# RMSNorm with SiLU on one core: three slots of eight rows instead of six of four, with loads on SyncE and stores on ScalarE

## The chip, the cores and the metric

The kernel runs on one core of a Trainium2 chip. The metric is the device time of one execution, in microseconds (us). Before the change three executions took 316.73, 316.79 and 317.04 us; the median, 316.79 us, is the time before.

The engines that matter here are VectorE (DVE in the profile), ScalarE (ACT), SyncE (SP, which only issues transfers) and the core's 16 DMA engines, which move data between the chip's DRAM and the on-chip memory. TensorE (PE) only spreads `gamma` over the partitions at the start.

## The reference

`x` is (8, 1024, 2048) in float32, that is 8192 rows of 2048 numbers. Each row is divided by its root mean square, multiplied by `gamma`, and passed through SiLU:

```python
rms = np.sqrt(np.mean(x ** 2, axis=-1, keepdims=True) + eps)
out = gamma * x / rms
return (out * (1 / (1 + np.exp(-out)))).astype(np.float32)
```

The input is 67.1 MB and so is the output. Both cross the DMA engines once.

## The kernel before

The 8192 rows are cut into 16 blocks of 512 rows. A block puts four neighbouring rows into each of the 128 partitions, so that a partition holds 4 x 2048 float32, 32 KB, and a block is 4 MB. Six such buffers (tile `xt`, `BUFS = 6`) fill most of the on-chip memory. A block is loaded, worked on in place and stored from the same buffer; a buffer is loaded again when its store has ended.

The work on a block `b`, row by row over a partition's four rows:

- `squares_scalar` (line 65) sums the squares of one or two rows on ScalarE, `squares_vector` (line 73) those of the others on VectorE; `share(b)` says how many go to ScalarE. The squares themselves go into scratch in PSUM (`junk_a`, `junk_v`), the sums into `ss`.
- `root` (line 82) takes the root of all four means in one ScalarE instruction, and `invert` (line 87) the reciprocal on VectorE (`rstd`).
- `multiply` (line 92) multiplies each row by its `rstd` and by `gamma` in one VectorE instruction per row.
- `silu` (line 98) applies SiLU on ScalarE to two rows at a time, and `store(b)` (line 102) then writes the whole block with one transfer, issued on SyncE's queue.

Square root and SiLU need different tables on ScalarE, so each change between them loads a table (ACT_TABLE_LOAD). The last block is different: its rows are multiplied by `gamma` alone (line 155) while the root is still on its way, and SiLU gets `rstd` as its scale (line 157).

Loads are issued by `load(b)` (line 54) on ScalarE's queue. Blocks 0 and 1 are issued at once, blocks 2 to 5 after `gamma` has been spread (line 116 makes ScalarE wait for that). From then on block `b + 3` is issued from inside `squares_scalar(b + 1)`. The order on every engine is the order in which the program is written (`manual_schedule`); the loop at line 128 interleaves block `b` and `b + 1` by hand.

`gamma` is loaded into one partition on SyncE's queue (line 110), spread by matmuls with a column of ones (line 113) and copied to `g` (line 115).

Of the kernel before, what the change touches and what calls it, by code (L numbers as in the profile page):

```python
# [1 line left out]

# [4 lines left out]

ACT = mybir.ActivationFunctionType
ALU = mybir.AluOpType


@with_exitstack
def kernel(
    ctx: ExitStack,
    tc: tile.TileContext,
    x: bass.AP,
    gamma: bass.AP,
    eps: bass.AP,
    out: bass.AP,
):  # L20

    nc = tc.nc
    P = nc.NUM_PARTITIONS
    f32 = mybir.dt.float32
    x2 = x.flatten_outer_dims()
    o2 = out.flatten_outer_dims()  # L30
    n, d = x2.shape
    J = 4
    BUFS = 6
    nblk = n // (P * J)
    xb = x2.rearrange("(b p j) d -> b p (j d)", p=P, j=J)
    ob = o2.rearrange("(b p j) d -> b p (j d)", p=P, j=J)

    singles = ctx.enter_context(tc.tile_pool(name="singles", bufs=1))
    pool = ctx.enter_context(tc.tile_pool(name="pool", bufs=BUFS))
    small = ctx.enter_context(tc.tile_pool(name="small", bufs=2))  # L40
    psum = ctx.enter_context(tc.tile_pool(name="psum", bufs=1, space=bass.MemoryType.PSUM))

    Q = 4
    w = d // Q
    g = singles.tile([P, d], f32)
    eps_t = singles.tile([P, 1], f32)
    ones = singles.tile([P, P], f32)
    junk_a = psum.tile([P, d], f32, name="junk_a")
    junk_v = psum.tile([P, d], f32, name="junk_v")
    blocks, sss, rmss, rstds = {}, {}, {}, {}  # L50
# [6 lines left out]
    def row(b, j):  # L57
        return blocks[b][:, j * d:(j + 1) * d]

    def squares_scalar(b, loads=()):  # L60


        sss[b] = small.tile([P, J], f32, name="ss")
        for j in range(share(b)):
            nc.scalar.activation(out=junk_a, in_=row(b, j), func=ACT.Square,  # L65
                                 accum_out=sss[b][:, j:j + 1])
            if j == 0:
                for s in loads:
                    load(s)

    def squares_vector(b):
        for j in range(share(b), J):
            nc.vector.tensor_tensor_reduce(  # L73
                out=junk_v, in0=row(b, j), in1=row(b, j), scale=1.0, scalar=0.0,
                op0=ALU.mult, op1=ALU.add, accum_out=sss[b][:, j:j + 1])

    def share(b):
        return 1 if 4 <= b <= 12 and b % 2 == 0 else 2

    def root(b):  # L80
        rms = small.tile([P, J], f32, name="rms")
        nc.scalar.activation(out=rms, in_=sss.pop(b), func=ACT.Sqrt, scale=1.0 / d, bias=eps_t)  # L82
        rmss[b] = rms

    def invert(b):
        rstd = small.tile([P, J], f32, name="rstd")
        nc.vector.reciprocal(out=rstd, in_=rmss.pop(b))  # L87
        rstds[b] = rstd

    def multiply(b):  # L90
        for j in range(J):
            nc.vector.scalar_tensor_tensor(out=row(b, j), in0=row(b, j), scalar=rstds[b][:, j:j + 1],  # L92
                                           in1=g, op0=ALU.mult, op1=ALU.mult)

    def silu(b):
        for h in range(0, J, 2):
            cols = slice(h * d, (h + 2) * d)
            nc.scalar.activation(out=blocks[b][:, cols], in_=blocks[b][:, cols], func=ACT.Silu)  # L98
        store(b)

    def store(b):
        nc.sync.dma_start(out=ob[b], in_=blocks[b])

    with tc.manual_schedule():

        load(0)
        nc.vector.memset(ones, 1.0)  # L107
        nc.vector.memset(eps_t, float(eps))
        nc.scalar.activation(out=junk_a[:, 0:1], in_=ones[:, 0:1], func=ACT.Square)  # L109
        nc.sync.dma_start(out=g[0:1, :], in_=bass.AP(tensor=gamma.tensor, offset=gamma.offset, ap=[[d, 1], [1, d]]))  # L110
        for c in range(Q):
            cols = slice(c * w, (c + 1) * w)
            nc.tensor.matmul(junk_v[:, cols], ones[0:1, :], g[0:1, cols], start=True, stop=True)  # L113
        load(1)
# [7 lines left out]
        last = nblk - 1  # L122
        SOON = 3
        squares_scalar(0)
        squares_vector(0)
        root(0)
        invert(0)
        for b in range(last):
            loads = [b + 3] if BUFS <= b + 3 < nblk else []
            if b < SOON:  # L130
                multiply(b)
                squares_scalar(b + 1, loads)
                silu(b)
                squares_vector(b + 1)
                root(b + 1)
            elif b < last - 1:
                squares_scalar(b + 1, loads)
                squares_vector(b + 1)
                root(b + 1)
                multiply(b)  # L140
                silu(b)
            else:
                multiply(b)
                squares_scalar(b + 1)
                silu(b)
                squares_vector(b + 1)
                root(b + 1)
            if b + 1 < last:
                invert(b + 1)


        for j in range(J):
            if j == J // 2:
                invert(last)
            nc.vector.tensor_mul(out=row(last, j), in0=row(last, j), in1=g)  # L155
        for j in range(J):
            nc.scalar.activation(out=row(last, j), in_=row(last, j), func=ACT.Silu,  # L157
                                 scale=rstds[last][:, j:j + 1])
        store(last)


# [33 lines left out]
```

## Time and profile before

| | before |
|---|---|
| time, median of three | 316.79 us (316.73 to 317.04) |
| span of the profiled execution, first to last instruction | 315.1 us |
| the median less that span | 1.69 us |
| VectorE busy | 235.3 us, 75% of the span |
| ScalarE busy | 213.9 us, 68% |
| moved by DMA | 134.24 MB, mean 426 GB/s |
| share of the 16 DMA engines: loads (q10), stores (q1) | 49.8%, 49.3% |

The profile gives no time of its own for the profiled execution beside its span; the 1.69 us are the start and end of a launch that lie outside the span. The page divides the span into 40 slices of 7.9 us and shows in tenths how busy each engine was. Queue q10 is the one of ScalarE and carries the loads, q1 is the one of SyncE and carries the stores and `gamma`; q14 fetches instructions. The trace also keeps a record of each DMA packet: its queue, its start, its length in time and its bytes. A block of 4 MB is 128 packets of 32768 bytes, one per partition, eight on each of the 16 engines, and a packet of 4 bytes on each engine behind them that signals the end.

### The profile page before, as it was taken

How to read it: one execution, taken by the hardware profiler on the slowest of the kernel's cores; microseconds unless marked ns; L12 is line 12 of the kernel's file. 1: busy time of each engine (PE TensorE's matmuls, PEld its weight loads, DVE VectorE, ACT ScalarE, POOL GpSimd, SP SyncE). 2: the span in 40 equal slices, each digit the busy share in tenths (PEclk: the TensorE clock that was granted, in tenths of full speed). 3: DMA queues.
4: the chain of work that ended last, by engine and by line, in shares of the span. 5: the costliest groups of instructions: out<-in, count | busy, mean ns of one | idle time of the engine just before them, and what ended most of it. 6: DMA issues, size and time to landing. Idle time of an engine off the chain costs nothing.

```text
span 315.1 us, 439 instructions
## 1 busy us (share of the span) xinstructions
PE 7.2 (2%) x8; PEld 2.5 (1%) x8; DVE 235.3 (75%) x157; ACT 213.9 (68%) x137; POOL 0.2 (0%) x4
## 2 busy tenths in 40 slices
PE   6200000000000000000000000000000000000000
PEld 2000000000000000000000000000000000000000
DVE  0679697979895695957969489593995939999600
ACT  1269998972799258682687827877278768779910
POOL 0000000000000000000000000000000000000000
DMA  8999999999999999999999999999999999999997
GB/s 334 412 453 416 383 458 408 462 403 462 403 459 408 454 412 458 408 462 403 462 403 462 408 458 408 458 408 458 416 449 416 449 416 449 428 437 428 437 428 308
DMA packets 4613, 134.24 MB, mean 426 GB/s; under 512 B 514, under 2 KB 514, under 8 KB 514
## 3 DMA queue, kind: packets, MB, share of 16 engines
q10 hardware_dynamic: 2304, 67.11, 49.8%
q1 hardware_dynamic: 2306, 67.12, 49.3%
q14 instruction: 3, 0.02, 0.0%
HBM read 67.12 MB, written 67.11 MB: 426 GB/s over the span
## 4 chain that ended last, share of the span: by engine, by line
DMA 68%; DVE 14%; ACT 11%; issue 1%; ACTq 1%; DVEq 0%
DMA xt<-in_x_dram 68%; DVE xt L92 9%; DVE junk_v L73 5%; ACT xt L98 4%; ACT junk_a L65 3%; ACT xt L157 2%; ACT L82 1%; ACTq L190 1%; ACT L157 0%; ACT L98 0%; ACT rms L82 0%; DVE ss L73 0%; ACTq L54 0%; DVE rstd L87 0%; ACT L109 0%
## 5 line engine op out<-in xcount | busy, mean ns | idle before, releaser
L92 DVE SCALAR_TENSOR_TENSOR xt<-xt,rstd,g 128x2048 f32<-128x2048 f32 x60 | 137.0, 2346 | 0.1
L98 ACT ACTIVATE xt<-xt 128x4096 f32<-128x4096 f32 x30 | 108.3, 3615 | 27.4 <-DVE xt L92 27.4
L73 DVE CUSTOM_DVE_ANT_0 junk_v<-xt 128x2048 f32<-128x2048 f32 x37 | 85.1, 2299 | 42.9 <-DMA xt<-in_x_dram 42.2
L65 ACT ACTIVATE junk_a<-xt 128x2048 f32<-128x2048 f32 x27 | 50.7, 1876 | 16.1 <-DMA xt<-in_x_dram 14.0
L82 ACT ACT_TABLE_LOAD x15 | 19.2, 1283 | 26.6 <-DVE ss L73 26.5
L98 ACT ACT_TABLE_LOAD x14 | 18.0, 1283 | 0.2
L115 DVE COPY g<-junk_v 128x2048 f32<-128x2048 f32 x1 | 2.3, 2292 | 9.0 <-PE junk_v L113 9.0
L87 DVE RECIPROCAL rstd<-rms 128x4 f32<-128x4 f32 x16 | 2.7, 172 | 8.4 <-ACT rms L82 8.4
L155 DVE TENSOR_TENSOR xt<-xt,g 128x2048 f32<-128x2048 f32 x4 | 8.9, 2277 | 0.0
L82 ACT ACTIVATE rms<-ss,eps_t 128x4 f32<-128x4 f32 x16 | 4.8, 297 | 5.7 <-DVE ss L73 5.5
L157 ACT ACTIVATE xt<-xt,rstd 128x2048 f32<-128x2048 f32 x4 | 7.7, 1991 | 0.0
L113 PE MATMUL junk_v<-g,ones 1*128 1x512 f32 x8 | 7.2, 1072 | 2.8 <-DMA g<-in_gamma_dram 2.8
L116 ACT COPY junk_a<-junk_v 128x1 f32<-128x1 f32 x1 | 0.1, 144 | 9.8 <-DVE g L115 9.8
L73 DVE DVE_READ_ACCUMULATOR2_ANT ss<- 128x1 f32 x37 | 5.2, 141 | 0.0
L65 ACT ACTIVATION_READ_ACCUMULATOR junk_a<-xt 128x1 f32 x27 | 5.0, 186 | 0.0
L113 PEld LDWEIGHTS junk_v<-g,ones 1*128 1x128 f32 x8 | 2.5, 325 | 5.9 <-issue 5.9
L109 ACT ACT_TABLE_LOAD x1 | 1.3, 1283 | 1.1 <-PEq L176 1.1
L157 ACT ACT_TABLE_LOAD x1 | 1.3, 1283 | 0.0
L107 DVE MEMSET ones<- 128x128 f32 x1 | 0.2, 165 | 0.8 <-PEq L176 0.8
L109 ACT ACTIVATE junk_a<-ones 128x1 f32<-128x1 f32 x1 | 0.2, 174 | 0.0
L176 POOL MEMSET const-bfloat16-1.0<- 128x1 bf16 x1 | 0.1, 103 | 0.0
L176 POOL MEMSET const-uint8-127<- 128x1 uint8 x1 | 0.1, 102 | 0.0
(3 smaller groups left out, 0.3 us busy)
## 6 DMA issues: line engine op xcount, KB each, us to landing
xt<-in_x_dram ACTq DMA_DIRECT2D x16, 4096.0 KB, 38.7
out_dram<-xt SPq DMA_DIRECT2D x16, 4096.0 KB, 29.0
g<-in_gamma_dram SPq DMA_DIRECT2D x1, 8.0 KB
```

What stands on the lines that cost most here:

```text
L65: nc.scalar.activation(out=junk_a, in_=row(b, j), func=ACT.Square, accum_out=sss[b][:, j:j + 1])
L73: nc.vector.tensor_tensor_reduce(out=junk_v, in0=row(b, j), in1=row(b, j), scale=1.0, scalar=0.0, op0=ALU.mult, op1=ALU.add, accum_out=sss ...
L82: nc.scalar.activation(out=rms, in_=sss.pop(b), func=ACT.Sqrt, scale=1.0 / d, bias=eps_t)
L87: nc.vector.reciprocal(out=rstd, in_=rmss.pop(b))
L92: nc.vector.scalar_tensor_tensor(out=row(b, j), in0=row(b, j), scalar=rstds[b][:, j:j + 1], in1=g, op0=ALU.mult, op1=ALU.mult)
L98: nc.scalar.activation(out=blocks[b][:, cols], in_=blocks[b][:, cols], func=ACT.Silu)
L109: nc.scalar.activation(out=junk_a[:, 0:1], in_=ones[:, 0:1], func=ACT.Square)
L113: nc.tensor.matmul(junk_v[:, cols], ones[0:1, :], g[0:1, cols], start=True, stop=True)
L115: nc.vector.tensor_copy(out=g, in_=junk_v)
L155: nc.vector.tensor_mul(out=row(last, j), in0=row(last, j), in1=g)
L157: nc.scalar.activation(out=row(last, j), in_=row(last, j), func=ACT.Silu, scale=rstds[last][:, j:j + 1])
L190: with _tile.TileContext(nc) as tc:
```

## The change

The rows are now described by a list, `FILLINGS`, of what goes into one slot. There are three slots of eight rows per partition (64 KB per partition, 8 MB), the same memory as six of four. Six fillings in the middle are one block of eight rows, loaded by one transfer in which a partition's eight rows are one run of 64 KB in DRAM. The first and the last filling are two blocks of four rows each, loaded as before. All stores take four rows: a middle block is stored in two transfers of 128 runs of 32 KB, which lie 64 KB apart in DRAM.

Loads are issued on SyncE's queue, and stores and `gamma` on ScalarE's. The first three fillings are all issued at the start without a wait; filling `k + 3` is issued once the stores of filling `k` have ended.

The blocks are no longer interleaved by hand. `compute(b)` is written out block after block: VectorE sums the squares of the first half of the rows, ScalarE of the second half; ScalarE takes the root; VectorE multiplies the rows by `gamma` alone and takes the reciprocal after the first of them; ScalarE applies SiLU row by row, with `rstd` as scale, and issues a store after each four rows. That is the form that only the last block had before.

The launch around the kernel is unchanged. The core of the diff:

```diff
+FILLINGS = [
+    [(4, 4), (4, 4)],
+    [(8, 4)],
...
+    [(8, 4)],
+    [(4, 4), (4, 4)],
+]
+SLOTS = 3
...
-    J = 4
-    BUFS = 6
-    nblk = n // (P * J)
-    xb = x2.rearrange("(b p j) d -> b p (j d)", p=P, j=J)
-    ob = o2.rearrange("(b p j) d -> b p (j d)", p=P, j=J)
+    ROWS = max(sum(j for j, _ in f) for f in FILLINGS)
...
-    pool = ctx.enter_context(tc.tile_pool(name="pool", bufs=BUFS))
-    small = ctx.enter_context(tc.tile_pool(name="small", bufs=2))
+    pool = ctx.enter_context(tc.tile_pool(name="pool", bufs=SLOTS))
+    small = ctx.enter_context(tc.tile_pool(name="small", bufs=3))
...
-    def load(b):
-        xt = pool.tile([P, J * d], f32, name="xt")
-        nc.scalar.dma_start(out=xt, in_=xb[b])
-        blocks[b] = xt
+    for f in FILLINGS:
+        blocks, r = [], 0
+        for j, per_store in f:
+            b = Block()
+            b.rows, b.per_store, b.offset = j, per_store, r
+            b.x = x2[at:at + j * P, :].rearrange("(p j) d -> p (j d)", p=P, j=j)
+            b.out = o2[at:at + j * P, :].rearrange("(p j) d -> p (j d)", p=P, j=j)
...
+    def load(b, slot):
+        b.slot = slot
+        nc.sync.dma_start(out=rows(b, 0, b.rows), in_=b.x)
+    def fill(k):
+        slot = pool.tile([P, ROWS * d], f32, name="xt")
+        for b in fillings[k]:
+            load(b, slot)
+    def rows(b, j, k=1):
+        return b.slot[:, (b.offset + j) * d:(b.offset + j + k) * d]
+    def compute(b):
+        J = b.rows
+        half = J // 2
...
+        for j in range(half):
+            nc.vector.tensor_tensor_reduce(
+                out=junk_v, in0=rows(b, j), in1=rows(b, j), scale=1.0, scalar=0.0,
+                op0=ALU.mult, op1=ALU.add, accum_out=ss[:, j:j + 1])
+        for j in range(half, J):
+            nc.scalar.activation(out=junk_a, in_=rows(b, j), func=ACT.Square,
+                                 accum_out=ss[:, j:j + 1])
+        nc.scalar.activation(out=rms[:, 0:J], in_=ss[:, 0:J], func=ACT.Sqrt, scale=1.0 / d, bias=eps_t)
+        for j in range(J):
+            nc.vector.tensor_mul(out=rows(b, j), in0=rows(b, j), in1=g)
+            if j == 0:
+                nc.vector.reciprocal(out=rstd[:, 0:J], in_=rms[:, 0:J])
+        for j in range(J):
+            nc.scalar.activation(out=rows(b, j), in_=rows(b, j), func=ACT.Silu,
+                                 scale=rstd[:, j:j + 1])
+            k = b.per_store
+            if (j + 1) % k == 0:
+                first = j + 1 - k
+                nc.scalar.dma_start(out=b.out[:, first * d:(j + 1) * d], in_=rows(b, first, k))
...
-        load(0)
+        slot = pool.tile([P, ROWS * d], f32, name="xt")
+        load(fillings[0][0], slot)
...
+        nc.scalar.dma_start(out=g[0:1, :], in_=bass.AP(tensor=gamma.tensor, offset=gamma.offset, ap=[[d, 1], [1, d]]))
         nc.scalar.activation(out=junk_a[:, 0:1], in_=ones[:, 0:1], func=ACT.Square)
-        nc.sync.dma_start(out=g[0:1, :], in_=bass.AP(tensor=gamma.tensor, offset=gamma.offset, ap=[[d, 1], [1, d]]))
...
-        load(1)
+        for b in fillings[0][1:]:
+            load(b, slot)
         nc.vector.tensor_copy(out=g, in_=junk_v)
-        nc.scalar.copy(out=junk_a[:, 0:1], in_=junk_v[:, d - 1:d])
-        for b in range(2, BUFS):
-            load(b)
...
+        for k in range(1, SLOTS):
+            fill(k)
+        for k in range(len(fillings)):
+            for b in fillings[k]:
+                compute(b)
+            if k + SLOTS < len(fillings):
+                fill(k + SLOTS)
```

More of the change, by code (lines that the diff above doesn't have):

```diff
@@ L9 @@
 ALU = mybir.AluOpType
+FILLINGS = [
+    [(4, 4), (4, 4)],
+    [(8, 4)],
+    [(8, 4)],
+    [(8, 4)],
+    [(8, 4)],
+    [(8, 4)],
+    [(8, 4)],
+    [(4, 4), (4, 4)],
+]
+SLOTS = 3
 @with_exitstack
@@ L31 @@
     n, d = x2.shape
-    J = 4
-    BUFS = 6
-    nblk = n // (P * J)
-    xb = x2.rearrange("(b p j) d -> b p (j d)", p=P, j=J)
-    ob = o2.rearrange("(b p j) d -> b p (j d)", p=P, j=J)
+    ROWS = max(sum(j for j, _ in f) for f in FILLINGS)
+    assert sum(j for f in FILLINGS for j, _ in f) * P == n
     singles = ctx.enter_context(tc.tile_pool(name="singles", bufs=1))
-    pool = ctx.enter_context(tc.tile_pool(name="pool", bufs=BUFS))
-    small = ctx.enter_context(tc.tile_pool(name="small", bufs=2))
+    pool = ctx.enter_context(tc.tile_pool(name="pool", bufs=SLOTS))
+    small = ctx.enter_context(tc.tile_pool(name="small", bufs=3))
     psum = ctx.enter_context(tc.tile_pool(name="psum", bufs=1, space=bass.MemoryType.PSUM))
@@ L49 @@
     junk_v = psum.tile([P, d], f32, name="junk_v")
-    blocks, sss, rmss, rstds = {}, {}, {}, {}
-    def load(b):
-        xt = pool.tile([P, J * d], f32, name="xt")
-        nc.scalar.dma_start(out=xt, in_=xb[b])
-        blocks[b] = xt
[L57 to L66, printed above, removed]
-            if j == 0:
-                for s in loads:
-                    load(s)
@@ L71, in squares_vector @@
[L71 to L90, printed above, removed]
-        for j in range(J):
[L92 to L99, printed above, removed]
@@ L101, in store @@
-    def store(b):
-        nc.sync.dma_start(out=ob[b], in_=blocks[b])
+    class Block:
+        pass
+    fillings, at = [], 0
+    for f in FILLINGS:
[5 more added lines that the diff above has]
+            b.out = o2[at:at + j * P, :].rearrange("(p j) d -> p (j d)", p=P, j=j)
+            blocks.append(b)
+            r += j
+            at += j * P
+        fillings.append(blocks)
@@ new lines, in load @@
+    def load(b, slot):
[10 more added lines that the diff above has]
+        half = J // 2
+        ss = small.tile([P, ROWS], f32, name="ss")
+        rms = small.tile([P, ROWS], f32, name="rms")
+        rstd = small.tile([P, ROWS], f32, name="rstd")
+        for j in range(half):
[8 more added lines that the diff above has]
+            nc.vector.tensor_mul(out=rows(b, j), in0=rows(b, j), in1=g)
+            if j == 0:
+                nc.vector.reciprocal(out=rstd[:, 0:J], in_=rms[:, 0:J])
+        for j in range(J):
+            nc.scalar.activation(out=rows(b, j), in_=rows(b, j), func=ACT.Silu,
[4 more added lines that the diff above has]
+                nc.scalar.dma_start(out=b.out[:, first * d:(j + 1) * d], in_=rows(b, first, k))
@@ L113 @@
             nc.tensor.matmul(junk_v[:, cols], ones[0:1, :], g[0:1, cols], start=True, stop=True)
-        load(1)
+        for b in fillings[0][1:]:
+            load(b, slot)
         nc.vector.tensor_copy(out=g, in_=junk_v)
-        nc.scalar.copy(out=junk_a[:, 0:1], in_=junk_v[:, d - 1:d])
-        for b in range(2, BUFS):
-            load(b)
[L122 to L159, printed above, removed]
+        for k in range(1, SLOTS):
[5 more added lines that the diff above has]
+                fill(k + SLOTS)
 _INS = ['x', 'gamma', 'eps']
```

## The prediction

> **What bounds the kernel now.** I read the page's slices first, to see whether an engine or the transfers are full.
>
> ```profile
> DVE  0679697979895695957969489593995939999600
> ACT  1269998972799258682687827877278768779910
> DMA  8999999999999999999999999999999999999997
> GB/s 334 412 453 416 383 458 408 462 403 462 403 459 408 454 412 458 408 462 403 462 403 462 408 458 408 458 408 458 416 449 416 449 416 449 428 437 428 437 428 308
> ```
>
> DVE and ACT have holes in nearly every slice; the DMA engines are at 9 from the second slice to the last but one. The windows query cuts this finer (columns: stretch, its length, busy time by engine, granted clock, DMA share, GB/s).
>
> ```profile
> 2.00:36.00 34.00, 7.16 (x8) 2.49 (x8) 20.95 (x14) 19.56 (x17) 0.00 (x0) 1.00 0.99 423
> 36.00:40.00 4.00, 0.00 (x0) 0.00 (x0) 3.17 (x3) 3.96 (x5) 0.00 (x0) 1.00 1.09 377
> 40.00:279.00 239.00, 0.00 (x0) 0.00 (x0) 193.53 (x129) 167.94 (x104) 0.00 (x0) 1.00 1.00 433
> 279.00:301.00 22.00, 0.00 (x0) 0.00 (x0) 17.46 (x11) 21.56 (x13) 0.00 (x0) 1.00 0.99 429
> 301.00:313.00 12.00, 0.00 (x0) 0.00 (x0) 0.00 (x0) 0.00 (x0) 0.00 (x0) 1.00 1.01 437
> ```
>
> For 239 us the 16 engines move 433 GB/s without a gap, and go on at that rate to 313 us, although the last load has landed at 278.9: the stores have a backlog to the end. The time is the bytes. Of the packet records, 3928 of the 4096 packets of 32768 bytes took 1.213 us, and successive starts on one engine are 1.210 us apart. An engine has 256 of them: 256 x 1.210 = 309.8 us. To this come the mean start of the first packets (2.05 us), their excess over 1.213 (0.54 us for each engine), the excess at 36 to 39 us (0.88 us, below) and 32 signals of 9 ns (0.29 us): 313.5 us. The engines end between 313.1 and 313.95, and the span is 315.1. No stretch is left in which the engines wait for work.
>
> Then the waits and, from the timeline, the end, to see how much slack stands behind the transfers.
>
> ```profile
> DVE junk_v L73 <- DMA xt<-in_x_dram: 42.2, 11, 5.7
> ACT xt L98 <- DVE xt L92: 27.4, 23, 2.8
> 290.30 1.28 ACT L82 ACT_TABLE_LOAD   x1
> 293.20 7.68 ACT L157 ACTIVATE xt<-xt,rstd 128x2048 f32<-128x2048 f32 x4
> ```
>
> DVE waits 42.2 us for loads, and ACT's last work ends at 300.9, 2.5 us before the store ahead of it leaves the queue (303.4). Compute is late nowhere; a change in it is worth nothing unless it makes the queues run dry.
>
> **Bytes and packets.** The bytes stay. Six middle loads of 64 KB runs replace twelve of 32 KB: per engine 6 x 8 = 48 packets of 65536 bytes for 96 of 32768, and six signals fewer. What a packet costs beyond its bytes comes from two records: 8192 bytes (instruction fetch at 89.4 us) took 309 ns and 32768 bytes 1213 ns, so 904 ns per 24576 bytes and 309 - 8192 x 904 / 24576 = 7.7 ns fixed. Then 65536 bytes take 2.418 us instead of 2.426, and the sum is 48 x 7.7 + 6 x 9 ns = 0.42 us off. The lower bound of this gain is 0 (the fixed part may not be one, or the run may be cut in two).
>
> **Pitch.** No row of before has a stride of 64 KB between partitions. Every row has 32 KB, in loads and stores, and both run at 1.213 us, so I take no cost; below, it could be a loss. The Trainium skill, page "DMA: Bandwidth & Descriptors", section "Latency and other measured facts", speaks against the change: at pitches of large powers of two it measured 207 GB/s at 512 KiB against 214 with a padded pitch. A loss of 3.4% on all 48 packets would be 3.9 us, an estimate from that page; 64 KB is not in its list and no run here shows it.
>
> **Who gets the DMA.** The records alternate one packet of q10, one of q1 while both have work. The same page (section "Queues, rings and completion order") says that a whole group of some 9 to 17 descriptors is drained before switching; here it is one 32 KB packet, and the trace decides. So 64 KB loads beside 32 KB stores get two thirds: a pair lasts 2.42 + 1.21 = 3.63 us, a middle load 8 x 3.63 = 29 us, in which one 4-row store goes too; its other store (9.7 us) then runs alone. A filling is 29 + 9.7 = 38.7 us, against two times 19.36 before: nothing lost, if the stores have backlog whenever the load queue is empty.
>
> **Compute of a middle block.** Squares on DVE: 4 x (2.299 + about 0.09 exposed of the accumulator read) = 9.6 us (L73); on ACT 4 x 2.04 = 8.2 (L65). Then the table 1.28 and root 0.30 (L82): 11.2 after the start. DVE multiplies row 0 meanwhile (2.28, L155), the reciprocal takes 0.17 (L87), the other seven 7 x 2.28 = 16. SiLU follows a row behind (1.99, L157): rows 0 to 3 end about 21 us after the landing, rows 4 to 7 about 30. DVE needs 9.6 + 18.2 + 0.2 = 28.0 us, ACT 8.2 + 2 x 1.28 + 0.3 + 8 x 1.99 + two store issues of 0.33 = 27.6; with the wait for the root between, about 30 of the 38.7 us. That is hidden with 8 us to spare. ACT's issues now stand among its work: behind each are four SiLUs or the next block's squares, and 2 x 0.33 us fits the same 8 us. SP only issues loads, so its wait for a slot holds up nothing but the next load.
>
> **Does a queue run dry?** I stepped the packets of one engine through both queues by these durations. The first stores are issued at about 29 and 44 us (35 and 50 before). Filling 2 lands at 75; slot 0 is free at 81, and from then on each load lands about 9 us before the next slot is free: fillings 3 to 7 start at about 82, 120, 159, 198 and 237. In these 9 us the stores carry the DMA: at a landing about 22 store packets are queued, 26 us of work, and the next store is issued after 21. At the end the last load lands at 277, its store is issued at 294 (301 before), and the queue has stores until 303.4. So the cover at the end is 9 us, at the landings some 17; 1.213 us is lost per 32 KB by which it fails. Slot releases later by 6 us left the end unmoved in the stepping.
>
> **Starts of a queue.** The excess of 0.88 us per engine at 36 to 39 us belongs to the first store: issued at 35.18, and until its packets start at 39.6 two load packets on each engine are stretched. The change keeps a first store, now beside 64 KB packets; 0 to 1.8 us, I keep 0.88. But the load queue, never empty before until 278 us, now runs empty and starts again five times beside busy stores. No load does that in the trace. The nearest rows are the two instruction fetches, a queue that starts from empty: their own 0.31 us and a stretch of 0.12 and 0.36 us of a store packet, on one engine; and the first store with 0.88 us on all. I take 0, because the first store is the first use of a queue for large transfers, and keep 0.88 for the range.
>
> **Sum.** 315.1 + 1.69 = 316.79; less 0.42 gives 316.37, so 316.4 us.
>
> **Rivals.**
> - *Each restart of the load queue costs DMA time* (slower). Five restarts at 0.12 to 0.36 us are 0.6 to 1.8 us: 317.0 to 318.2. At 0.88 they are 4.4 us: 320.8. It decides from (0.42 + 0.63) / 5 = 0.21 us each. For: both kinds of start in the trace stretched the neighbour's packets. Against: both were either first uses or another kind of queue. Chance 0.30.
> - *The 64 KB pitch slows a packet* (slower). At 1% on 48 packets of 2.418 us it is 1.2 us, 317.5. For: nothing in the trace; against: both directions run at one rate at 32 KB. Chance 0.07.
> - *The run is cut into 32 KB packets.* Then queues share evenly and the packets are the old ones: 316.8. Chance 0.07.
> - *The first store's stretch goes or is halved* (faster): 315.5 to 315.9. For: its cause is not known, and it comes earlier. Chance 0.08.
> - *A queue runs dry at the end*: it needs the last compute 9 us later than worked out, a third more than a whole middle block needs on DVE; each us beyond that is 1 us. I give it no chance of its own.
>
> **How the numbers follow.** My forecast, DMA full and packets a little cheaper, has 0.48, and its own range is 316.0 to 316.7, by the 0 to 0.42 us of the packets and the 0.4 us by which the engines' ends differ. The bound of 0.2% is 0.63 us, about what a measurement can tell here: faster is below 316.16, slower above 317.42. The forecast gives faster 0.14 and same 0.34; the restarts give slower 0.25 and same 0.05; the pitch slower 0.07; the cut run same 0.05, faster 0.02; the stretch faster 0.08. Summed: faster 0.24, same 0.44, slower 0.32. The range goes from 315.9 to 319.5, which is 316.37 and five restarts at 0.62 us, the middle between 0.36 and 0.88.
>
> **What would show it.** Right: 768 load packets of 65536 bytes at about 2.418 us, 433 GB/s from 40 us to the end, load and store packets one by one, load landings near 112, 151, 190 and 228, the last store issued near 294 with stores before it until 303. Wrong: stretched packets within 4 us of 82, 120, 159, 198 or 237 (restarts), a packet of 64 KB above 2.43 us throughout (pitch), a DMA share below 0.99 in a window between 40 and 300 us (a dry queue), or only 32 KB packets.

## The result and the profile after

The changed kernel takes 317.45 us (median of 16 runs, 317.07 to 317.85) against 316.81 us of the kernel before in the same sessions (16 runs, 316.67 to 317.36). By the medians it is 0.64 us slower, where 0.4 us faster was forecast; the ratio goes by the means and is 1.0017, interval 1.001 to 1.0024, or 0.54 us (0.3 to 0.8). The profiled execution took 317.67 us; its span is 315.9 us against 315.1.

First the slices of its page, which answer to those of before.

```profile
DVE  0699829997999139990499904999059998849200
ACT  1389959898899338993479824799258989958500
DMA  8999999999999999999899999999999999999996
GB/s 333 407 456 465 373 423 432 432 436 427 463 407 494 419 394 465 402 436 490 361 444 419 490 407 407 440 419 477 407 432 411 452 407 456 419 444 416 456 407 278
```

DVE now has one deep hole in each 38.7 us (slices 14, 19, 24 and 29, counted from 1): a middle block is worked on in 30 us and then both engines wait for the next landing. The DMA engines are full as before. The windows query, with the cuts used for before (stretch, length, busy time by engine, clock, DMA share, GB/s):

```profile
2.00:36.00 34.00, 7.16 (x8) 2.48 (x8) 23.70 (x17) 22.10 (x20) 0.00 (x0) 1.00 1.02 428
36.00:40.00 4.00, 0.00 (x0) 0.00 (x0) 4.00 (x3) 3.99 (x4) 0.00 (x0) 1.00 1.10 475
40.00:279.00 239.00, 0.00 (x0) 0.00 (x0) 177.54 (x112) 178.45 (x128) 0.00 (x0) 1.00 1.00 430
279.00:301.00 22.00, 0.00 (x0) 0.00 (x0) 13.53 (x9) 14.66 (x11) 0.00 (x0) 1.00 1.02 441
301.00:313.00 12.00, 0.00 (x0) 0.00 (x0) 0.00 (x0) 0.00 (x0) 0.00 (x0) 1.00 0.95 410
313.00:315.90 2.90, 0.00 (x0) 0.00 (x0) 0.00 (x0) 0.00 (x0) 0.00 (x0) 1.00 0.05 23
```

(Packets are counted whole where they start, so a stretch can show more than it moved.) Up to 301 us the share is 1.00 or more. The loss is in the last two lines: from 301 to 313 us the share is 0.95, and some of it is still at work after 313. No engine waits for a store to be issued; the timeline shows the last one in good time.

```profile
287.62 6.66 DVE L99 TENSOR_TENSOR xt<-xt,g 128x2048 f32<-128x2048 f32 x3
288.44 7.87 ACT L103 ACTIVATE xt<-xt,rstd 128x2048 f32<-128x2048 f32 x4
296.34 0.34 ACTq L108 DMA_DIRECT2D out_dram<-xt  x1
```

The last store is issued at 296.3 and its first packets start behind the store before it, at 303. So some DMA engines finish early and some late. The packet records tell this engine by engine, by the 16 signals that end the last store:

```
end of the last store on the 16 DMA engines (us)
            first    mean     last    last - first
before     313.12   313.44   313.96      0.84
after      312.67   313.38   314.57      1.89
```

The mean engine is 0.06 us earlier. The slowest is 0.61 us later, and the time follows the slowest. In the 16 profiled experiments below the time of the profiled execution is the end of the slowest DMA engine plus 2.93 to 3.19 us, from 316.9 to 380 us. Of each kernel one execution was profiled, so these ends are those of a single execution each.

How the mean comes about, each term summed over the packets of all engines and divided by 16: the plain duration of the packets falls from 310.53 to 310.14 us (-0.38) and six signals go (-0.05), as worked out; the first packets start 0.07 earlier and are stretched 0.08 more; the first store stretches its neighbours by 0.70 instead of 0.88 us; one instruction fetch more is 0.02; and stretched packets after 42 us are 0.42 us instead of 0.03. Together that is -0.19; the rest, about 0.1 us of small gaps, is not itemized. The 0.42 us lie on few packets, 32 over 30 ns: 0.57 us (behind an instruction fetch) and 0.53 us near 86 us, 0.39 and 0.86 at 164.6, five of 0.30 to 0.42 at 203 to 204. The engine that ends last took a fetch at 81.7 us with 0.19 us of stretch behind it, 0.97 us at 163 to 165 and 0.37 at 182 to 190. The third fetch, at 289.7 us, falls on an engine that ends near 313.1 us, so in this execution it is not what made the last engine late. An engine's number is not in the records; it is followed by matching ends to starts, which can exchange two engines whose packets end within a few ns.

### The profile page after: what moved, and what is told of

Its sections match the earlier page's. It is cut to its first block, busy times and chain, and to the rows that moved or that the text cites. A ratio compares the mean times of both kernels' runs of the same rounds, so it can differ in the third digit from the quotient of the medians.

```text
span 315.9 us, 425 instructions
## 1 busy us (share of the span) xinstructions
PE 7.2 (2%) x8; PEld 2.5 (1%) x8; DVE 218.9 (69%) x141; ACT 219.9 (70%) x160; POOL 0.2 (0%) x4
## 4 chain that ended last, share of the span: by engine, by line
DMA 42%; another core or an unknown queue 37%; DVE 13%; ACT 1%; SPq 1%; issue 0%; DVEq 0%
DMA xt<-in_x_dram 28%; DMA out_dram<-xt 14%; DVE xt L99 8%; DVE junk_v L91 4%; ACT xt L103 1%; SPq L74 1%; DVE ss L91 0%; DVE rstd L101 0%; DVEq L160 0%
## 5 line engine op out<-in xcount | busy, mean ns | idle before, releaser
L99 DVE TENSOR_TENSOR xt<-xt,g 128x2048 f32<-128x2048 f32 x64 | 142.2, 2278 | 0.0
L103 ACT ACTIVATE xt<-xt,rstd 128x2048 f32<-128x2048 f32 x64 | 125.7, 1997 | 5.7 <-DVE xt L99 4.9
L91 DVE CUSTOM_DVE_ANT_0 junk_v<-xt 128x2048 f32<-128x2048 f32 x32 | 73.6, 2300 | 64.1 <-DMA xt<-in_x_dram 63.4
L95 ACT ACTIVATE junk_a<-xt 128x2048 f32<-128x2048 f32 x32 | 60.2, 1882 | 58.9 <-DMA xt<-in_x_dram 56.9
L95 ACT ACTIVATION_READ_ACCUMULATOR junk_a<-xt 128x1 f32 x32 | 6.0, 186 | 0.0
L91 DVE DVE_READ_ACCUMULATOR2_ANT ss<- 128x1 f32 x32 | 4.5, 141 | 0.0
L97 ACT ACTIVATE rms<-ss,eps_t 128x8 f32<-128x8 f32 (+1 forms) x10 | 3.0, 299 | 0.1
L101 DVE RECIPROCAL rstd<-rms 128x8 f32<-128x8 f32 (+1 forms) x10 | 1.9, 186 | 1.4 <-ACT rms L97 1.4
```

The costliest lines, as they stand in the source:

```text
L91: nc.vector.tensor_tensor_reduce(out=junk_v, in0=rows(b, j), in1=rows(b, j), scale=1.0, scalar=0.0, op0=ALU.mult, op1=ALU.add, accum_out=s ...
L95: nc.scalar.activation(out=junk_a, in_=rows(b, j), func=ACT.Square, accum_out=ss[:, j:j + 1])
L97: nc.scalar.activation(out=rms[:, 0:J], in_=ss[:, 0:J], func=ACT.Sqrt, scale=1.0 / d, bias=eps_t)
L99: nc.vector.tensor_mul(out=rows(b, j), in0=rows(b, j), in1=g)
L101: nc.vector.reciprocal(out=rstd[:, 0:J], in_=rms[:, 0:J])
L103: nc.scalar.activation(out=rows(b, j), in_=rows(b, j), func=ACT.Silu, scale=rstd[:, j:j + 1])
```

## The experiments

Each ran beside the kernel before on the same chip, but not all of them on one chip and in one session; so two experiments are best compared by what each is over its own "before". "Mean" and "last" are the ends of the DMA engines in the profile; "fetches" are the records of 8192 bytes on q14 after the start.

| | median us (before) | ratio, interval | mean, last us | fetches |
|---|---|---|---|---|
| before | 316.81 | | 313.44, 313.96 | 2 |
| after | 317.45 (316.81) | 1.0017, 1.001 to 1.0024 | 313.38, 314.57 | 3 |
| e1_even64 | 320.64 (316.87) | 1.0125, 1.0102 to 1.0148 | 316.50, 318.68 | 3 |
| e2_halves | 317.41 (316.87) | 1.002, 1.0011 to 1.0028 | 313.40, 314.24 | 3 |
| e3_restart32 | 322.01 (316.87) | 1.0172, 1.0159 to 1.0185 | 315.34, 317.66 | 3 |
| e4_six | 318.02 (316.87) | 1.0052, 1.0029 to 1.0074 | 313.72, 314.77 | 3 |
| e5_pairs | 317.22 (316.89) | 1.0012, 1.0003 to 1.0021 | 313.41, 313.78 | 2 |
| e6_halves_quads | 380.11 (316.89) | 1.1994, 1.1978 to 1.2011 | 376.94, 377.03 | 2 |
| e7_pool450 | 318.65 (316.89) | 1.0071, 1.0043 to 1.0099 | 314.40, 315.54 | 6 |
| e8_pool1600 | 323.58 (316.89) | 1.0207, 1.0193 to 1.0221 | 319.42, 320.43 | 15 |
| e9_act30 | 317.07 (316.94) | 1.0003, 0.9995 to 1.0012 | 313.46, 313.94 | 3 |
| e10_mixed_pairs | 322.44 (316.94) | 1.0164, 1.0142 to 1.0185 | 317.63, 320.17 | 2 |
| e11_six_pairs | 317.88 (316.94) | 1.0035, 1.0023 to 1.0047 | 314.11, 316.77 | 3 |
| e12_swap | 317.28 (316.91) | 1.001, 1.0002 to 1.0019 | 313.24, 314.23 | 2 |
| e13_cut | 317.94 (316.91) | 1.0038, 1.0024 to 1.0051 | 313.68, 315.05 | 3 |
| e14_slots6 | 317.28 (316.91) | 1.0014, 1.0005 to 1.0022 | 313.29, 314.12 | 3 |
| e15_unswap | 317.73 (316.94) | 1.0023, 1.0012 to 1.0034 | 313.39, 313.98 | 3 |
| e16_swap_pool450 | 318.65 (316.94) | 1.005, 1.0037 to 1.0063 | 313.47, 315.70 | 6 |

### First round: long packets, starts of a queue, or the rest of the change

Theory A was the rival of the prediction (each start of the empty load queue costs DMA time), sharpened by the ends of the engines; theory B blamed the long packets themselves, theory C the slots, queues and order of the work.

**e1_even64**

```diff
-    [(8, 4)],
+    [(8, 8)],
```

(all six middle fillings)

> Middle blocks are stored in one transfer of 64 KB runs instead of two of 32 KB; all else is as in the changed kernel. Load and store packets are then equally long, loads get half of the DMA and no longer run ahead; stepped through, the load queue runs empty twice (near 75 and 197 us) instead of five times. Packets per engine fall from 208 to 160. Theory A (each start of the empty load queue beside busy stores stretches the first packets of a few engines, and the engine that has lost most sets the end): the engines end within 1.4 us of each other instead of 1.89, the mean end falls by 48 x 7.7 ns = 0.4 us, time 316.3 to 316.9. Theory B (packets of 64 KB themselves drift the engines apart): still a spread of 1.9 us or more, as twice as many packets are long, time 317.2 or more. Theory C (the slots of eight rows, the queues or the order of the work cost it): 317.4 as the changed kernel.

320.64 us, far outside what A and C had; B's open range (317.2 or more) holds it, but for another reason. The last store was issued only at 305.65 us, and the queue had run dry; the windows around it:

```profile
300.00:304.00 4.00, 0.00 (x0) 0.00 (x0) 3.58 (x2) 3.92 (x3) 0.00 (x0) 1.00 0.67 287
304.00:307.00 3.00, 0.00 (x0) 0.00 (x0) 0.00 (x0) 1.62 (x1) 0.00 (x0) 1.00 0.51 218
```

A store of eight rows goes out 9 us later than its first half could, and that uses up the cover at the end. The run doesn't tell A from B.

**e2_halves**

```diff
-    [(8, 4)],
+    [(4, 4), (4, 4)],
```

(all six)

> All fillings are two blocks of four rows, loaded and stored in 32 KB runs; three slots of eight rows, queues and order of work as in the changed kernel. Stepped through, the load queue never runs empty before the last load. Theory A: engines end within about 0.85 us as in the kernel before, time 316.6 to 317.0, like before. Theory B: the same, as no packet is over 32 KB. Theory C: 317.4, as slots, queues and order stay changed.

317.41 us. No packet over 32 KB, no start of the load queue after 31 us, and yet the time of the changed kernel: theory C by the time. In the records a cause stands out that no theory had: the two latest engines (314.12 and 314.24 us, the next one is at 313.57) are those that took instruction fetches, one at 78.5 us, the other at 78.2 and 255.5. Behind each a packet is stretched, by 0.58, 0.30 and 0.32 us.

**e3_restart32**

```diff
-FILLINGS = [ ... ]
+FILLINGS = [[(4, 2), (4, 2)]] * 8
```

> All fillings are two blocks of four rows in 32 KB loads, and stores take two rows, 16 KB runs. Loads again get two thirds of the DMA and, stepped through, run empty and start again five times (near 85, 124, 163, 201 and 240 us), without any packet of 64 KB. 128 more store packets per engine than with 32 KB stores cost 128 x 7.7 ns = 1.0 us of mean. Theory A: stretched packets just after the five starts, engines end 1.5 us or more apart, time 318.0 to 318.8. Theory B: engines end within 0.9 us, time 317.6 to 317.9. Theory C: as A by time, but without stretched packets at the starts.

322.01 us. The load queue started from empty at 85.8, 124.4, 164.5, 204.0 and 243.8 us, as stepped, and around four of them packets of all sizes were stretched: summed and divided by 16, 0.24, 0.54, 0.28 and 0.05 us, none at the first. No packet was over 32 KB. So a start can cost without long packets, which is against B; it costs more here than A had it (the profiled execution, 320.62 us, is even the fastest of five).

**e4_six**

```diff
-SLOTS = 3
+FILLINGS = [[(4, 4)]] + [[(6, 6)]] * 9 + [[(4, 4), (2, 2)]]
+SLOTS = 4
```

> Four slots of six rows (the same memory), blocks of six rows loaded and stored each in one transfer of 48 KB runs; first block four rows, last filling four and two rows. Loads and stores are equally long, and stepped through the load queue never runs empty and no store is late at the end (last store issued at 303 with others before it). 176 packets per engine instead of 256 in the kernel before: 80 x 7.7 ns = 0.6 us less. Theory A: engines end within 0.9 us, time 316.0 to 316.4, faster than both. Theory B (drift grows with the size of a packet): spread 1.2 us or more, time 316.7 or more. Theory C (slots over four rows, queues, order): 317 or more.

318.02 us, runs from 317.45 to 320.38: a miss for A. The last store was issued at 305.8 us, 3 us later than stepped, and at 86.7 us, as a load was to be issued (87.6), five engines had a load packet stretched by 0.38 to 0.47 us. So larger blocks brought late engines of their own without a long gap in either queue; by what, the run does not say.

### Second round: the instruction fetches

Theory F: each engine reads its program in pieces, over q14. In the records ScalarE's second piece comes when it has executed 60 to 66 of its records, the next near 190 (188 to 194); the kernel before has 177 on ScalarE, the changed one 202. The page's count of q14 hides this, since it also counts a record of 32 bytes.

**e5_pairs**

```diff
+        if J == 8:
+            nc.vector.reciprocal(out=rstd[:, 0:J], in_=rms[:, 0:J])
+            for j in range(J):
+                nc.vector.scalar_tensor_tensor(out=rows(b, j), in0=rows(b, j), scalar=rstd[:, j:j + 1],
+                                               in1=g, op0=ALU.mult, op1=ALU.mult)
+            for j in range(0, J, 2):
+                nc.scalar.activation(out=rows(b, j, 2), in_=rows(b, j, 2), func=ACT.Silu)
...
```

> The changed kernel, but middle blocks multiply by rstd and gamma in one VectorE instruction and apply SiLU to two rows at a time, as the kernel before does; 24 instructions fewer on ScalarE (178 in place of 202 records). Loads, stores and slots stay. Theory F (each fetch of the next 8 KB of an engine's program takes 0.31 us of one DMA engine and stretches the packet behind it, 0.4 to 0.9 us in all; ScalarE fetches again after about 190 records, and that third fetch, which the kernel before does not have, is what made the last DMA engine late): two fetches instead of three, time 316.6 to 317.0. Theory A (the five starts of the empty load queue made it late): two fetches, but the spread of the engines' ends stays 1.5 us or more by stretched packets near 85, 124, 164 and 204 us, time 317.2 to 317.6.

317.22 us, between the two: 0.33 over before, where the changed kernel is 0.64 over its own (0.23 under it by the medians alone), and its interval overlaps that of the changed kernel and just leaves out 1. The profiled execution was the fastest of eleven (316.88); in it the spread is 0.96 us and the stretches near 164 and 203 us are there, but fall on other engines than the two fetches.

**e6_halves_quads**

```diff
+        if b is not fillings[-1][-1]:
...
+            for j in range(0, J, 4):
+                nc.scalar.activation(out=rows(b, j, 4), in_=rows(b, j, 4), func=ACT.Silu)
```

> As e2_halves (blocks of four rows in 32 KB runs, no start of the load queue), but all blocks save the last apply SiLU to four rows in one instruction and multiply by rstd on VectorE; about 183 ScalarE records in place of 228. Theory F: two fetches instead of three, engines end within about 0.85 us, time 316.6 to 317.0, 0.4 us under e2_halves. If slots, queues or order of the work cost the 0.6 us (theory C): 317.4 again.

380.11 us, for a reason of its own: with SiLU on all four rows at once, ScalarE waits for the last multiply and VectorE for the next root, and the two take turns (22.5 us per block).

```profile
ACT xt L95 <- DVE xt L92: 121.8, 15, 8.1
DVE rstd L90 <- ACT rms L88: 120.7, 15, 8.5
```

Each waits some 120 us for the other, as these waits (total, times, longest) show. Nothing on theory F follows.

**e7_pool450 and e8_pool1600**

```diff
         nc.vector.memset(eps_t, float(eps))
+        for _ in range(450):
+            nc.gpsimd.memset(idle, 0.0)
```

(1600 in e8_pool1600; `idle` is a new one-column tile)

> The kernel before with 450 one-column memsets on GpSimd at the start, into a tile that nothing reads; nothing else changes and GpSimd is idle in both. Theory F: three or four more fetches of 8 KB in the first 60 us, each 0.31 us of a DMA engine and 0.1 to 0.6 us of stretch; where they fall on engines that are late already the end moves, 317.0 to 317.6. Otherwise (fetches cost nothing): 316.8.

> As e7_pool450 with 1600 memsets: about twelve more fetches. Theory F: 12 x 0.4 to 0.9 us of DMA engine time on 16 engines, the unluckiest engine two or three of them, 317.6 to 319. Otherwise: 316.8.

318.65 and 323.58 us. The DMA page of e8_pool1600 shows how little it takes: 13 fetches of 8 KB by GpSimd, beside the two that the kernel before has, among 134 MB.

```profile
q10 hardware_dynamic: 2304, 67.11, 48.8%
q1 hardware_dynamic: 2306, 67.12, 48.5%
q14 instruction: 15, 0.12, 0.1%
```

All 13 of GpSimd's fetches fell on one DMA engine. Each takes 0.31 us there (one took 0.39), and the packet behind it is stretched by 0.09 to 0.35. At each landing that engine's signal comes further behind the first one: 4.13 us at 64 us, 5.93 at 122, 8.03 at 200, 9.61 at 258, (9.61 - 4.13) / 10 = 0.55 us for each of the ten fetches between, and nothing of it comes back. The late engine still carries eight packets of every one of these transfers, as the others do. The expectation had spread the fetches over the engines and was too low. Such an engine also holds up the others: a load has landed when its slowest engine is done, so compute and the next issues shift, and at the end the other 15 run out of work, for 5.5 us on the mean:

```profile
40.00:279.00 239.00, 0.00 (x0) 0.00 (x0) 186.24 (x124) 163.58 (x103) 132.42 (x1348) 1.00 1.00 432
279.00:301.00 22.00, 0.00 (x0) 0.00 (x0) 21.93 (x15) 19.15 (x12) 0.00 (x0) 1.00 0.80 343
301.00:313.00 12.00, 0.00 (x0) 0.00 (x0) 3.28 (x2) 7.68 (x4) 0.00 (x0) 1.00 0.92 396
313.00:321.70 8.70, 0.00 (x0) 0.00 (x0) 0.00 (x0) 0.00 (x0) 0.00 (x0) 1.00 0.71 305
```

The share is 1.00 until 279 us and 0.80 after it.

**e9_act30**

```diff
         load(1)
+        for _ in range(30):
+            nc.scalar.activation(out=junk_a[:, 0:1], in_=ones[:, 0:1], func=ACT.Square)
         nc.vector.tensor_copy(out=g, in_=junk_v)
```

> The kernel before with 30 one-column activations more on ScalarE, put where it waits for gamma at the start (it is idle there for 9.8 us). ScalarE then has 207 records in place of 177 and passes the 190th, as the changed kernel does. Theory F: one fetch more, near 280 us, on the DMA engine that ScalarE's first fetch used; that engine ends 0.4 to 0.7 us later, time 317.1 to 317.5. If the third fetch is harmless: 316.9.

317.07 us, 0.13 over before, and the interval holds no difference (-0.16 to +0.38 us). The third fetch came, at 268.6 us, with 0.12 us of stretch. A single fetch costs its engine 0.4 us, but that engine need not be the last.

### Third round: fewer starts

**e10_mixed_pairs**

```diff
-    [(8, 4)],
+    [(8, 8)],
```

(the first three middle fillings, on top of e5_pairs)

> As e5_pairs (two fetches), but three of the six middle blocks are stored in one transfer of 64 KB runs, so that loads run ahead less; stepped through, the load queue starts from empty three times instead of five (near 85, 201 and 240 us) and the store queue once more (158 us), and the last store is issued in time (near 296 us). Theory A: fewer starts, time 316.6 to 317.1, under e5_pairs. If starts cost nothing: 24 packets fewer per engine, 0.2 us under e5_pairs, with the same spread.

322.44 us. The first 64 KB store was issued at 81.2 us, as the queues had just run dry:

```profile
78.00:82.00 4.00, 0.00 (x0) 0.00 (x0) 3.97 (x3) 3.58 (x2) 0.00 (x0) 1.00 0.61 262
82.00:84.00 2.00, 0.00 (x0) 0.00 (x0) 1.97 (x3) 1.97 (x3) 0.00 (x0) 1.00 1.24 524
84.00:92.00 8.00, 0.00 (x0) 0.00 (x0) 3.56 (x6) 7.89 (x9) 0.00 (x0) 1.00 1.16 394
```

All engines stood still for 0.9 to 1.6 us, and then, with both queues starting at once, lost 1.98 us on the mean to stretched packets. At 161 us the load queue had just ended (161.1), the store queue started from empty and the next load was issued (161.5): 0.73 us on the mean, on the first store packet of 15 engines. At 204 us the load queue started beside a busy store queue: 0.16 us on the mean, nearly all of it on three engines (0.68 to 0.97). So where both queues start, the price is about that of the first store or more, and where the load queue starts alone, it is lower. The expectation for the whole was missed, because it had neither the dry queues at 81 us nor a price for the starts.

**e11_six_pairs**

```diff
-SLOTS = 3
+FILLINGS = [[(4, 4)]] + [[(6, 6)]] * 6 + [[(6, 2)]] * 3 + [[(4, 4), (2, 2)]]
+SLOTS = 4
...
+        if J == 6:
```

(then as in e5_pairs)

> Four slots of six rows, loads of 48 KB runs; six blocks stored in 48 KB runs, the last three in 16 KB runs so that loads finish early; SiLU on two rows, so that ScalarE stays under 190 records. Stepped through, no queue runs empty between 31 us and the last load, and the last store is issued near 297 us with 8 us of others before it. Theories F and A together: two fetches, no starts, fewer packets (about 0.3 us less): 316.4 to 316.9, as fast as the kernel before or faster. If slots or size of packets cost something by themselves: 317.2 or more.

317.88 us, a miss. The load queue did not start from empty after 42 us, but in the profiled execution (319.86 us, the slowest of twelve) two engines end at 316.54 and 316.77 us and the next at 314.86. One of the two fell behind by 0.25 to 0.50 us in each 29 us (85.3, 114.6, 143.9, 173.3, 202.6, 226.6 us), the first five times right behind the signal that ends a store. At 234 to 241 us load packets on eleven engines were stretched as well, 0.19 us on the mean. The third fetch, at 319.0, comes after the last store has ended and costs nothing. Why one engine is hit each time, I could not find out.

### Fourth round: the parts of the change by themselves

**e12_swap**

```diff
-        nc.scalar.dma_start(out=xt, in_=xb[b])
+        nc.sync.dma_start(out=xt, in_=xb[b])
...
-        nc.sync.dma_start(out=ob[b], in_=blocks[b])
+        nc.scalar.dma_start(out=ob[b], in_=blocks[b])
```

(in the kernel before; `gamma` goes to ScalarE too)

> The kernel before with the queues exchanged: loads on SyncE, stores and gamma on ScalarE; block sizes, slots and order of the work stay. Loads are then issued as soon as their slot is free instead of from inside the squares. Theory A (starts of the load queue and the long packets that cause them): no starts, 316.7 to 317.1. Theory Q (the exchange itself costs, as e2_halves was 0.5 us over the kernel before without any start): 317.3 to 317.6.

317.28 us: with the queues exchanged and nothing else edited the kernel is 0.37 us slower (0.06 to 0.60 by the ratio). The loads are also issued some 6 us earlier here (118.7 in place of 124.5 us, for one), so the run measures the exchange and the time of issue together. The mean engine ends 0.20 us earlier than before, the last 0.27 us later. It is the one with the fetch at 108.9 us, which has 0.54 us of stretch behind it; in the kernel before the fetch at 108.8 has 0.36. The other fetch has 0.25 here and 0.12 there. In both profiles the packet behind a fetch belongs to q1: a store before, a load now.

**e13_cut**

```diff
-        nc.sync.dma_start(out=rows(b, 0, b.rows), in_=b.x)
+        for j in range(0, b.rows, 4):
+            nc.sync.dma_start(out=rows(b, j, 4), in_=b.x[:, j * d:(j + 4) * d])
```

> The changed kernel with its middle loads cut into two transfers of 32 KB runs (four rows each, 64 KB apart in DRAM); blocks, slots, order, stores and queues stay. Loads and stores share evenly, so that, stepped through, the load queue never starts from empty; the store queue runs empty once (70 to 75 us) and starts again. The 0.4 us of the longer packets is lost. Theory A: no stretched packets near 124, 163, 202 and 240 us; the gain of the missing starts and the loss of 0.4 us nearly cancel, less 0 to 0.7 us for the one start of the store queue: 317.2 to 317.9, engines' ends within 1.3 us. If starts cost nothing: 0.4 us over the changed kernel, 317.9, with stretched packets at the same times.

317.94 us, 1.03 over before, where the changed kernel is 0.64 over its own; its interval (1.0024 to 1.0051) just touches the other. The load queue never ran empty after 42 us and the clusters of 0.3 to 0.9 us at 164 and 204 are gone. In their place are stretches of up to 0.15 us on four to six engines every 38.7 us (96 to 99, 135, 174, 213, 252), and one engine ended at 315.05. The one start of the store queue cost 0.07 us on the mean: a packet on each of four engines was stretched by 0.17 to 0.37 us at 70 us. The mean end is 0.30 us later than in the changed kernel, which is about what the 64 KB packets had saved. The time lies where "starts cost nothing" had put it, and the spread of the ends (1.86 us) is over the 1.3 us of A; the missing clusters are as A had them. For the starts the run is inconclusive; with the gain of the packets it agrees.

**e14_slots6**

```diff
-SLOTS = 3
+FILLINGS = [[(4, 4)]] * 16
+SLOTS = 6
```

> As e2_halves, but six slots of four rows instead of three of eight, so that each block's slot is released by itself as in the kernel before. Queues, order of the work, packets and the third fetch stay. If the coarse release of two blocks together costs (theory C, slots): 316.9 in place of 317.4. Otherwise 317.4.

317.28 us, within the runs of e2_halves (317.21 to 318.48). The slots of eight rows and their joint release cost nothing that can be seen.

**e15_unswap**

```diff
-        nc.sync.dma_start(out=rows(b, 0, b.rows), in_=b.x)
+        nc.scalar.dma_start(out=rows(b, 0, b.rows), in_=b.x)
...
-                nc.scalar.dma_start(out=b.out[:, first * d:(j + 1) * d], in_=rows(b, first, k))
+                nc.sync.dma_start(out=b.out[:, first * d:(j + 1) * d], in_=rows(b, first, k))
...
-            if k + SLOTS < len(fillings):
-                fill(k + SLOTS)
+            if k >= 3 and k - 3 + SLOTS < len(fillings):
+                fill(k - 3 + SLOTS)
```

(in e14_slots6)

> As e14_slots6 (the changed kernel's order of work, six slots of four rows, no start of the load queue, three fetches), but with the queues as in the kernel before: stores and gamma on SyncE, loads on ScalarE, where block k + 3 is issued after the work of block k, late enough not to wait. Theory Q (with the loads on SyncE's queue the packet behind a fetch is a load and is stretched by 0.25 to 0.58 us; with the stores there it is a store, 0.09 to 0.36): packets behind the fetches stretched by about 0.12 and 0.36 us, time 316.9 to 317.1. If the exchange has nothing to do with it: 317.3 as e14_slots6.

317.73 us, with runs from 316.85 to 318.52: wider than any of the others of this structure, and no gain. The profiled execution was a quick one (316.99) and shows the three fetches as expected, with 0.12, 0.35 and 0.19 us behind them, and the last engine at 313.98 us. So taking the exchange out of e14_slots6 did not make it faster: 0.79 us over before against 0.37. What the slower of its runs lost is not in a profile.

**e16_swap_pool450**

```diff
-        nc.scalar.dma_start(out=xt, in_=xb[b])
+        nc.sync.dma_start(out=xt, in_=xb[b])
...
```

(the exchange of e12_swap in e7_pool450)

> The kernel before with the queues exchanged (e12_swap) and the 450 memsets on GpSimd of e7_pool450, which bring four more fetches to one DMA engine. Theory Q: the same four fetches cost more than with the stores on SyncE's queue, 0.31 + 0.25 to 0.58 us each instead of 0.31 + 0.09 to 0.36: 319.2 to 320.2, over 318.65 of e7_pool450. If the exchange does not change what a fetch costs: 1.76 us over e12_swap at the most, 318.6 to 319.0.

318.65 us, the same as e7_pool450 (1.71 us over before against 1.76): theory Q fails as a rule for every fetch. GpSimd's four have 0.22 to 0.35 us behind them here and 0.09 to 0.35 there; only those of ScalarE and VectorE (0.25 and 0.53) are dearer with the loads on q1.

## Why the prediction was wrong

**What held.** The DMA engines are the bound and stay full. A packet of 64 KB takes 2.418 us: 714 of 768 did, at 64 KB between partitions, so the pitch costs nothing here. (The Trainium skill, page "DMA: Bandwidth & Descriptors", section "Latency and other measured facts", has losses for much larger pitches only; no run here reaches those.) Load and store packets alternate one by one, and the stepping of the two queues was right to within 4 us:

| | stepped | measured |
|---|---|---|
| loads of fillings 3 to 7 issued (us) | 82, 120, 159, 198, 237 | 81.6, 120.8, 159.5, 198.9, 237.5 |
| fillings 3 to 6 landed | 112, 151, 190, 228 | 115, 154, 194, 232 |
| last store issued | 294 | 296.3 |

The DMA engines never ran out of work before the end, and compute was hidden. What e13_cut gave back (0.39 us by the differences from before) fits the 0.42 us of the packets. The time lies in the whole range of 315.9 to 319.5 us, but only because that range was made wide for the rival; the forecast's own range, 316.0 to 316.7, misses it.

**The step that failed** is the sum. It took 0.42 us off the time, as if the end were that of the mean engine; the ends' differences appeared in it only as a fixed 0.4 us of the range. The mean engine's end moved by -0.06 us, and the time by +0.64, because the slowest engine's end moved by +0.61. Each DMA engine has a fixed share of every transfer, no other takes over what it has not done, and what it loses it keeps: in e8_pool1600 the late engine carries its eight packets of each load, while its lag grows from 4.13 to 9.61 us.

**The terms that were priced wrongly**, as far as the runs tell:
- The exchange of the queues had no term at all. In the kernel before it costs 0.37 us, 0.06 to 0.60, together with the earlier issue of the loads (e12_swap).
- A third instruction fetch was not seen, although the prediction used fetches as its nearest rows and ScalarE's number of instructions can be counted from the diff. It costs 0.13 us in e9_act30, and 0.2 to 0.3 is what e5_pairs brings, which is without it; neither is clear of zero alone, and in the profile of the changed kernel it falls on an early engine.
- The starts of the load queue were taken at 0 and kept at up to 0.88 us each for the rival. The sign that the prediction had named for them is there, stretched packets at 86 to 87, 124, 165 and 203 to 204 us. On the mean engine the five cost 0.08 (half of it behind two fetches), 0.01, 0.09, 0.12 and 0.00 us, 0.3 together; on a single engine up to 0.97 at once. The rival's price was near for single engines and too high for the mean; its range for the time, 317.0 to 318.2, holds the result.
- The first store's stretch was kept at 0.88 us and came out at 0.70, in favour of the mean. The profile of e5_pairs, which starts in the same way, has 0.93 us, and all profiles together 0.63 to 1.22, so this is luck and no gain of the change.

The first two together, some 0.5 us, are as large as what e2_halves and e14_slots6 lose (0.54 and 0.37 us over before), which have the exchange and the third fetch but neither long packets nor starts. That they are the cause is not shown, since e15_unswap, without the exchange, is not faster. The changed kernel has long packets and starts besides and takes about the same time: the packets' gain of about 0.4 us is used up, perhaps by the stretched packets after the starts. That step is an inference from the records; no run took the starts away and kept the 64 KB loads with all else equal (e1_even64, e10_mixed_pairs and e11_six_pairs, which were to do it, each brought another loss), and e13_cut, which has neither long packets nor starts of the load queue, ends with a still later engine.

**What stays open.** Which of the terms made the last engine late in most executions, as each kernel has one profile. Whether and why the exchange costs: the dearer packet behind the fetches is in the profile of e12_swap, but e15_unswap, which removes it, is not faster, and e16_swap_pool450, which multiplies fetches, is not slower than without the exchange. And why a stretch falls on single engines, in e11_six_pairs on the same one six times.

## What to carry to other kernels

Where the DMA engines are full from start to end, a change in the time is a change of the slowest of the 16, not of their mean: look at the spread of the signals that end a transfer before a gain in bytes or packets is booked. Count the instructions on each engine, since every further piece of program is read by the same DMA engines; and count how often a queue starts from empty beside a busy one. A queue that was never empty before has no row in the trace for that price, and the nearest rows, the first store and the fetches, were the right ones to take at more than nothing, if less than their own price: 0.06 us for each start on the mean engine here.

## What had not been expected of the hardware

- An instruction fetch of 8 KB costs the DMA engine that carries it 0.31 us and the packet behind it 0.09 to 0.65 us more (0.86 at 88 us in e10_mixed_pairs, where both queues started). GpSimd's 13 fetches in e8_pool1600 all fell on one DMA engine, 0.55 us each, and the kernel became 6.7 us slower by 0.1 MB.
- Packets are stretched when a queue starts from empty, at a price that differs much. On the mean engine it was 0.70 to 0.88 us at the first store in before and after (load packets), 0.73 and 1.98 us where both queues start (e10_mixed_pairs), 0.07 us for the store queue in e13_cut, and 0.00 to 0.12 us for the load queue in the changed kernel, there mostly on its own first packet on a few engines (in e3_restart32 up to 0.54).
- One engine that lags holds back landings for all: in e8_pool1600 15 engines stood still for 5.5 us on the mean toward the end, for an engine that was 9.6 us late.
